# First modulation as columns on TensorE, norm and skip on the Hyena filters, and a new load order in front of a hybrid encoder layer

## The chip, the cores and the metric

The kernel runs on one core of one Trainium2 chip. The metric is the device time of one execution in microseconds (us), less is better. The kernel before takes 1514.09 us, the median of three runs (1512.0 to 1516.69).

## What is computed

One layer of an encoder trunk over 1024 tokens of width 1024, cut to what matters here:

```
sh1, sc1, g1, sh2, sc2, g2 = split(silu(c) @ mod_w + mod_b)     # six vectors of 1024
u  = rms_norm(x) * (1 + sc1) + sh1
p  = u @ w_in                     # 28 tiles of 128 columns and 24 gate columns
SSD, NA, mLSTM, Hyena each work on their columns of p
x  = x + g1 * (concat(groups) @ w_out)
x  = x + g2 * SwiGLU(rms_norm(x) * (1 + sc2) + sh2)
out = rms_norm(x)
# Hyena: per order o two filters h = sin-MLP(features) @ w3 * decay,
# divided by the root of their square sum; y = fft-convolution(z, h) + skip * z
```

Only the first two of the six vectors, sh1 and sc1, are needed in front of u. All is fp32. A product of the projection is made as three fp32r matmuls, hi·hi, lo·hi and hi·lo, of operands that are split into a rounded part and the rest.

## The kernel before

The program is one stream per engine, in order; the framework sorts each engine's instructions by priority and by when their operands come, and semaphores hold an instruction back until its operands are there. What stands behind a waiting instruction on its engine waits too.

The part in front is one function, `start` (L400 to L468), with the generator `hyena_filters` (L719) run beside it:

- **First modulation.** `mod_w` for sh1 and sc1 comes as four quarters q of 2 MB, each in four tiles `mw` of 512 KB. For q = 0 to 2 VectorE (DVE) multiplies a 128x512 slice of a tile by one element of silu(c) per partition and adds it to `acc` (L422, L424: 24 instructions); for q = 3 ScalarE (ACT) multiplies (L427) and GpSimd (POOL) adds (L429). Then 16 TensorE (PE) transposes (L449) and four reductions on DVE (L451) sum over the partitions and leave the result as columns in `mod1`.
- **Norm and split.** Eight 512 KB tiles of x come after all of `mw`. ACT squares them (L439), `rsqrt` on the sums makes the factors, L444 multiplies. For each half h of the tokens and each of eight column tiles k, PE transposes four 128x128 blocks (L462), ACT applies the modulation (L464, `tm`), and `split` makes `hhi` and `hlo` (L235, L239), the latter on DVE or POOL by turns.
- **Projection.** `gemm_t` (L485) makes one column tile of p transposed, 2 halves of 24 matmuls (L495, `gps`); `w_group` (L471) loads and splits the weights (`raw`, `whi`, `wlo`). The first three groups of tiles belong to Hyena: `conv3` (L512) and `to_natural` (L525, `nps`, `z`) follow them.
- **Filters.** `hyena_mlp` (L693) makes h2 with two sines (DVE polynomials L684 to L689, ACT L690). `hyena_filters` makes, for each order o and block j, a product with w3 on PE (L738, `fps`), times the decay `dc` on DVE (L743, `hf`), its square on ACT (L746), a sum of the two directions on DVE (L747), a matmul with ones that adds up the squares (L748, `nps`), and the sum and difference `hp`, `hm` on DVE (L751, L752). `dft16_fwd` (L536) runs a first stage of the transform on DVE (L550 to L607), `emit` the second on PE (L765, L767, `kps`), and then DVE multiplies each of the spectra by the norm (L769) and adds the skip to the real ones (L771) before they are stored in `kspec`.

The Hyena convolution (`fps` of L792) begins when z and the spectra are there. Behind it come the other groups, the second modulation (L1500, `mxw`), the out projection, the feed-forward part (`ffn`, products `X`, `Y`, `Z` of L1606 with combinations on DVE) and the last norm.

Of the kernel before, what the change touches and what calls it, by code (L numbers as in the profile page):

```python
# [9 lines left out]
F32 = mybir.dt.float32  # L10
F32R = mybir.dt.float32r
AF = mybir.ActivationFunctionType
ALU = mybir.AluOpType
# [7 lines left out]
NK = 8  # L21
# [197 lines left out]
class Net:  # L219


    def __init__(self, nc, tc, d, out):
        self.nc, self.tc, self.d, self.out = nc, tc, d, out
        self.n = 0

# [60 lines left out]
def build(nc, tc, d, out, dbg=None, dump=None):  # L286
    K = Net(nc, tc, d, out)
    with ExitStack() as es:
# [58 lines left out]
        with ExitStack() as e2:  # L347
# [3 lines left out]
            with ExitStack() as e3:  # L351
                fl = Tags(rpool("fl", e3), n4=2, n2=8, yk=3, n1=2, tab=3, ks=3)
                hyena_mlp(K, fl)
                K.wp = Tags(pool("wp", e2), raw=3, whi=2, wlo=2)
                with ExitStack() as e4:
                    hf = hyena_filters(K, fl)
                    w0 = []
                    start(K, hp, Tags(pool("st", e4), tm=2), lambda: next(hf), lambda: w0.extend(w_group(K, G_HY + 2, first=False)))
                for _ in hf:
                    pass  # L360
# [39 lines left out]
def start(K, hp, sp, between, mid):  # L400
# [3 lines left out]

    accs, mts = {}, {}
    slots = [f"{t}{k}" for k in range(NK) for t in ("hhi", "hlo")]
    for qs in ((0, 3), (1,), (2,)):
        if qs == (2,):
            between()
        for q in qs:  # L410
            accs[q] = sp.tile([P, 512], F32, f"acc{q}")
        for k in range(NK):
            for q in qs:

                acc, c = accs[q], K.cond[:, k:k + 1]
                if k % 2 == 0:
                    mts[q] = hp.tile([P, 2, 512], F32, name="mw", tag=slots.pop(0))
                    nc.sync.dma_start(mts[q], d["modw1"][q, :, k:k + 2].rearrange("p k s c -> p k (s c)"))
                w = mts[q][:, k % 2]
                if q < 3:  # L420
                    if k == 0:
                        V.tensor_scalar_mul(acc, w, c)  # L422
                    else:
                        V.scalar_tensor_tensor(acc, in0=w, scalar=c, in1=acc, op0=ALU.mult, op1=ALU.add)  # L424
                else:
                    t = acc if k == 0 else sp.tile([P, 512], F32, "pr", bufs=2)
                    nc.scalar.activation(t, w, AF.Identity, scale=c)  # L427
                    if k > 0:
                        nc.gpsimd.tensor_tensor(acc, acc, t, op=ALU.add)  # L429
    ss = sp.tile([P, 8], F32, "ss")  # L430
    xs = []
    for g in range(4):
        xt = K.wp.tile([P, NK, 288], F32, ("whi", "wlo")[g % 2], name="x").rearrange("p a b -> p (a b)")
        for i in range(2):
            x = xt[:, i * D:(i + 1) * D]
            n = 2 * g + i
            nc.sync.dma_start(x, d["x"][n * P:(n + 1) * P, :])
            jk = K.so.tile([P, D], F32, "st", name="jk")
            nc.scalar.activation(jk, x, AF.Square, accum_out=ss[:, n:n + 1])  # L439
            xs.append(x)  # L440
    def norm(h):
# [4 lines left out]
    for q in (0, 3, 1, 2):  # L446
        ps = K.pm.tile([P, 512], F32, tag="m", name="psm")
        for n in range(4):
            nc.tensor.transpose(ps[:, n * P:(n + 1) * P], accs[q][:, n * P:(n + 1) * P], K.ident)  # L449
        mc = sp.tile([P, 2, 2], F32, "mc", bufs=2)  # L450
        V.tensor_reduce(mc, ps.rearrange("p (s k x) -> p s k x", s=2, k=2), axis=AX.X, op=ALU.add)  # L451
        mv = K.mod1.rearrange("p (s k) -> p s k", s=2)[:, :, 2 * q:2 * q + 2]
        V.tensor_tensor(mv, mc, K.pc[:, PC_MODB:PC_MODB + 16].rearrange("p (s k) -> p s k", s=2)[:, :, 2 * q:2 * q + 2], op=ALU.add)
        V.tensor_scalar_add(mv[:, 1], mv[:, 1], 1.0)
    K.hhi = [hp.tile([P, L], F32R, name=f"hhi{k}", tag=f"hhi{k}") for k in range(NK)]
    K.hlo = [hp.tile([P, L], F32R, name=f"hlo{k}", tag=f"hlo{k}") for k in range(NK)]
    for h in range(2):
        norm(h)
        for k in range(NK):
# [3 lines left out]
            t = sp.tile([P, 512], F32, tag="tm") if k % 2 else K.so.tile([P, 512], F32, "st", name="tm")  # L463
# [21 lines left out]
def gemm_t(K, whi, wlo, j):  # L485
# [3 lines left out]
    pss = []  # L489
    for h in range(2):  # L490
# [3 lines left out]
        for n, (w, x, k) in enumerate(seq):  # L494
            nc.tensor.matmul(ps, lhsT=w[:, k, c], rhs=x[k][:, t], start=n == 0, stop=n == len(seq) - 1)  # L495
# [196 lines left out]

def hyena_mlp(K, sp):  # L693
# [7 lines left out]
    for c in range(2):  # L701
        nc.sync.dma_start(w2[64 * c:64 * c + 64], d["w2"])

# [15 lines left out]
def hyena_filters(K, sp):  # L719
# [4 lines left out]
    for o in range(2):  # L724
        w3 = sp.tile([P, 512], F32, "w3")
        for c in range(2):
            nc.sync.dma_start(w3[64 * c:64 * c + 64], d["w3"][:, o * 512:(o + 1) * 512])
        hp = sp.tile([P, 8, 256], F32, "hp")
        hm = sp.tile([P, 8, 256], F32, "hm")
        pn = K.pm.tile([P, 512], F32, "m", name="nps")[:, :256]  # L730
        pss = {}
        for j in (0, 4, 1, 5, 2, 6, 3, 7):
            if j < 4:

                for b in (j, j + 4):
                    r = slice(64 * (b // 4), 64 * (b // 4) + 64)
                    pss[b] = K.pm.tile([P, 512], F32, "m", name="fps")
                    nc.tensor.matmul(pss[b], lhsT=h2[r, j * P:(j + 1) * P], rhs=w3[r], start=True, stop=True)  # L738
            ps = pss[j]
            dc = sp.tile([P, 1, 256], F32, "n1", name="dc")  # L740
            nc.sync.dma_start(dc[:, 0], d["c_decay"][:, j])
            hf = sp.tile([P, 2, 256], F32, "n2", name="hf")
            V.tensor_tensor(hf, ps.rearrange("p (a b) -> p a b", a=2), dc.broadcast_to([P, 2, 256]), op=ALU.mult)  # L743
            hff = hf.rearrange("p a b -> p (a b)")
            s1 = sp.tile([P, 512], F32, "n2", name="s1")
            nc.scalar.activation(s1, hff, AF.Square)  # L746
            V.tensor_tensor(s1[:, 0:256], s1[:, 0:256], s1[:, 256:512], op=ALU.add)  # L747
            nc.tensor.matmul(pn, lhsT=K.ones, rhs=s1[:, 0:256], start=j == 0, stop=j == 7)  # L748
            if j == 0:
                G.memset(hf[0:1, 1, :], 0.0)  # L750
# [4 lines left out]
        fsc = K.rsqrt(sp, pn, [P, 256], 1.0, "fn")  # L755
        skip = sp.tile([P, 256], F32, "skip")
        nc.sync.dma_start(skip, d["skip"][:, 256 * o:256 * o + 256].broadcast_to([P, 256]))
        for q, (src, la, lb) in enumerate(((hp, 0, 1), (hm, 1, 0))):

            def emit(k, y):  # L760
# [821 lines left out]
def ffn(K, sp, S, at):  # L1582
# [134 lines left out]
    for f in range(NF):  # L1717
# [24 lines left out]
        if f < KH:  # L1742
            V.tensor_tensor(x[:, 0], x[:, 1], x[:, 0], op=ALU.subtract)
# [14 lines left out]
        if f < KH:  # L1758
            V.tensor_tensor(y[:, 1], a[:, 0:H], a[:, H:L], op=ALU.subtract)
# [118 lines left out]
```

## Time and profile before

| | us |
|---|---|
| median of three runs | 1514.09 (1512.0 to 1516.69) |
| profiled execution | 1520.79 |
| its span | 1518.9 |
| PE busy in the span | 1389.5 (91%) |
| DVE busy in the span | 1118.4 (74%) |
| ACT busy in the span | 542.5 (36%) |
| POOL busy in the span | 90.9 (6%) |
| first matmul of the projection | 85.82 |
| first matmul of the Hyena convolution | 218.86 |

The span runs from the first to the last recorded instruction of the profiled execution; that execution's own time is 1.9 us longer. A busy share is an average over the whole span. PE is busy for 36.90 of the first 85.80 us and for 1232.16 of the 1300 us behind 218.9. The granted clock is 1.00 for TensorE at its full speed of 2.4 GHz and 0.50 for the lower level of 1.2 GHz; a value between them is a stretch that has some of both.

### The profile page before, as it was taken

How to read it: one execution, taken by the hardware profiler on the slowest of the kernel's cores; microseconds unless marked ns; L12 is line 12 of the kernel's file. 1: busy time of each engine (PE TensorE's matmuls, PEld its weight loads, DVE VectorE, ACT ScalarE, POOL GpSimd, SP SyncE). 2: the span in 40 equal slices, each digit the busy share in tenths (PEclk: the TensorE clock that was granted, in tenths of full speed). 3: DMA queues.
4: the chain of work that ended last, by engine and by line, in shares of the span. 5: the costliest groups of instructions: out<-in, count | busy, mean ns of one | idle time of the engine just before them, and what ended most of it. 6: DMA issues, size and time to landing. Idle time of an engine off the chain costs nothing.

```text
span 1518.9 us, 19510 instructions
## 1 busy us (share of the span) xinstructions
PE 1389.5 (91%) x6717; PEld 1115.8 (73%) x6717; DVE 1118.4 (74%) x2123; ACT 542.5 (36%) x973; POOL 90.9 (6%) x143
## 2 busy tenths in 40 slices
PE   2589989998998998999998999999999999999995
PEld 0366768776787767877776777887778878888884
DVE  7999977887756684687865458378777887557588
ACT  2522221232142342333545766322222222434352
POOL 2110000000101231320000000000000000000000
PEclk9789999999998999989999999999999999999998
DMA  6634366577662324476435448677776776977762
GB/s 248 196 101 146 121 198 217 181 240 222 205 195 93 114 84 154 118 250 223 151 102 180 146 164 285 230 258 249 254 246 218 234 266 239 331 236 244 238 221 110
DMA packets 160598, 300.31 MB, mean 198 GB/s; under 512 B 27871, under 2 KB 72831, under 8 KB 160500
## 3 DMA queue, kind: packets, MB, share of 16 engines
q1 hardware_dynamic: 137204, 271.77, 54.6%
q10 hardware_dynamic: 22688, 25.99, 4.8%
q0 software_dynamic: 608, 1.31, 0.3%
q8 instruction: 53, 0.87, 0.2%
q14 instruction: 45, 0.37, 0.1%
HBM read 221.12 MB, written 77.89 MB: 197 GB/s over the span
## 4 chain that ended last, share of the span: by engine, by line
PE 59%; DVE 14%; DMA 9%; issue 3%; ACT 1%; POOL 1%; SPq 0%; POOLq 0%; DVEq 0%; ACTq 0%
PE Z L1606 8%; PE X L1606 6%; PE dx L1844 6%; PE Y L1606 5%; PE gps L495 5%; PE gps L507 4%; PE dz L1844 4%; PE dy L1844 4%; PE gps L1556 3%; DMA mxw<-modw 3%; DMA wu<-wu 2%; PE nS L1429 2%; PE ops L1556 1%; PE nS L1407 1%; DVE wlo L239 1%
## 5 line engine op out<-in xcount | busy, mean ns | idle before, releaser
L495 PE MATMUL gps<-hhi,whi 128*128 128x512 f32 x320 | 130.3, 407 | 3.8 <-ACT nt L531 3.8
L495 PE MATMUL gps<-hlo,whi 128*128 128x512 f32 x320 | 128.9, 403 | 0.0
L495 PE MATMUL gps<-hhi,wlo 128*128 128x512 f32 x320 | 128.4, 401 | 0.0
L239 DVE TENSOR_TENSOR dl<-dr,dh 128x1024 fp32r<-128x1024 f32 x77 | 93.5, 1221 | 37.4 <-ACT dh L233 25.2
L233 ACT CAST dh<-dr 128x1024 fp32r<-128x1024 f32 x77 | 80.4, 1052 | 104.6 <-PE dz L1844 30.0
L1606 PE MATMUL Z<-hp,wgh 128*128 128x512 f32 x352 | 95.8, 402 | 1.0 <-ACT ps L1661 0.9
L507 PE MATMUL gps<-whi,hhi 128*128 128x256 f32 (+1 forms) x256 | 76.8, 300 | 1.5 <-ACT z L531 1.5
L1606 PEld LDWEIGHTS Z<-hp,wgh 128*128 128x128 f32 x352 | 63.6, 188 | 19.2 <-ACT ps L1661 4.7
L507 PE MATMUL gps<-whi,hlo 128*128 128x256 f32 (+1 forms) x256 | 76.8, 300 | 0.0
L507 PE MATMUL gps<-wlo,hhi 128*128 128x256 f32 (+1 forms) x256 | 76.3, 298 | 0.0
L495 PEld LDWEIGHTS gps<-hhi,whi 128*128 128x128 f32 x320 | 60.5, 189 | 19.3 <-ACT nt L531 5.0
L233 ACT CAST T3h<-wu 128x1024 fp32r<-128x1024 f32 x22 | 23.1, 1052 | 132.0 <-PE Y L1606 121.1
L495 PEld LDWEIGHTS gps<-hhi,wlo 128*128 128x128 f32 x320 | 60.2, 188 | 13.7 <-issue 1.6
L495 PEld LDWEIGHTS gps<-hlo,whi 128*128 128x128 f32 x320 | 60.4, 189 | 12.2 <-issue 0.8
L1500 DVE SCALAR_TENSOR_TENSOR mxacc<-mxw,cond,mxacc 128x512 f32<-128x512 f32 x56 | 41.9, 748 | 32.4 <-DMA mxw<-modw 32.2
L1606 PE MATMUL X<-A,t4s 128*128 128x512 f32 x264 | 63.6, 390 | 0.1
L1606 PEld LDWEIGHTS X<-A,t4s 128*128 128x128 f32 x264 | 49.5, 188 | 10.8 <-DVE uv L1745 0.5
L507 PEld LDWEIGHTS gps<-whi,hhi 128*128 128x128 f32 x256 | 49.9, 195 | 3.1 <-ACT z L531 1.9
L1606 PE MATMUL Y<-AS,T3h 128*128 128x512 f32 x176 | 45.5, 400 | 7.3 <-DVE uv L1741 7.3
L1844 PE MATMUL dx<-dh,dl 128*128 128x512 f32 x132 | 51.4, 389 | 0.0
L1844 PE MATMUL dx<-dh 128*128 128x512 f32 x132 | 51.4, 389 | 0.0
L1844 PE MATMUL dx<-dl,dh 128*128 128x512 f32 x132 | 51.4, 389 | 0.0
(521 smaller groups left out, 3511.2 us busy)
## 6 DMA issues: line engine op xcount, KB each, us to landing
wg<-wg SPq DMA_DIRECT2D x44, 512.0 KB
mxw<-modw SPq DMA_DIRECT2D x64, 256.0 KB
raw<-w_in SPq DMA_DIRECT2D x28, 512.0 KB
dr<-wd SPq DMA_DIRECT2D x55, 256.0 KB
psd<-ps SPq DMA_DIRECT2D x22, 512.0 KB
psr<-psd SPq DMA_DIRECT2D x22, 512.0 KB
wu<-wu SPq DMA_DIRECT2D x22, 512.0 KB
ad<-a SPq DMA_DIRECT2D x22, 512.0 KB
```

Source lines behind the costliest of these rows:

```text
L233: nc.scalar.copy(hi, src)
L239: e.tensor_tensor(lo, src, hi.bitcast(F32), op=ALU.subtract)
L495: nc.tensor.matmul(ps, lhsT=w[:, k, c], rhs=x[k][:, t], start=n == 0, stop=n == len(seq) - 1)
L507: nc.tensor.matmul(ps, lhsT=x[k][:, t], rhs=w[:, k, :N], start=n == 0, stop=n == len(seq) - 1)
L1407: nc.tensor.matmul(pb[:, :nk], lhsT=qt[r, i], rhs=ktv[r, r0:r0 + nr, f * 24:f * 24 + 40], start=True, stop=True)
L1429: nc.tensor.matmul(pb[:, 448:512], lhsT=pT[:w * 40, n], rhs=vw[:w * 40, n, c:c + 64], start=n == 0, stop=n == len(chunks) - 1)
L1500: V.scalar_tensor_tensor(acc, in0=mt, scalar=K.cond[:, k:k + 1], in1=acc, op0=ALU.mult, op1=ALU.add)
L1556: K.nc.tensor.matmul(ps, lhsT=l, rhs=r, start=n == 0, stop=n == 5)
L1606: nc.tensor.matmul(ps, lhsT=w[a][:, k], rhs=x[k][b], start=start and n == 0, stop=n == 11, skip_group_check=not start)
L1844: nc.tensor.matmul(acc[i], lhsT=a[:, 0, ts], rhs=b[:, 1], start=first and m == 0, stop=final and m == 2, skip_group_check=n in (2, 3, 5, 6))
```

## The change

Four parts.

1. **Modulation on TensorE.** The accumulation on DVE, ACT and POOL is gone. For each quarter q, 32 matmuls (128 in all) take a 128x128 block of `mw` as the stationary operand and one column of silu(c) as the moving one, and write one column of `pc` each; a reduction over eight columns and the bias follow.
2. **Load order and halves.** On the load queue: w3 with the other filter weights, then x0 to x3, the whole decay as one transfer of 1 MB, the 16 tiles of `mw`, x4 to x7, w_in. The norm of half 0 stands ahead of the filters, that of half 1 behind the splits of half 0. `mid` hands its weights back, and half 0 of the column tiles j = 0 and 1 is multiplied before half 1 is transposed (`K.half`). All `hlo` are made on DVE, `tm` has three buffers.
3. **Filters.** Sum and difference of the two directions' weights are formed once per order (`ws`), so that the product with them is already hp or hm; the squares of both go to the matmul with ones, twice as many of them, and the factor 1.0 of `rsqrt` is 2.0. Norm and skip are applied to the filters, and the spectra are copied out by ACT.
4. **Feed-forward.** The two subtractions into `x` and the store `td` stand at the end of a column tile in the source.

```diff
-    for qs in ((0, 3), (1,), (2,)):
...
-                if q < 3:
-                    if k == 0:
-                        V.tensor_scalar_mul(acc, w, c)
-                    else:
-                        V.scalar_tensor_tensor(acc, in0=w, scalar=c, in1=acc, op0=ALU.mult, op1=ALU.add)
...
+    load_x(0)
+    nc.sync.dma_start(K.dc, d["c_decay"])
...
+            nc.sync.dma_start(mt, d["modw1"][q, :, 2 * n:2 * n + 2].rearrange("p k s c -> p k (s c)"))
+    load_x(1)
+    norm(0)
+    between()
+    for q in range(4):
+        pc = K.pm.tile([P, 512], F32, tag="m", name="psm")[:, 0:32]
+        for k in range(NK):
+            for c in range(4):
+                n = c * NK + k
+                nc.tensor.matmul(pc[:, n:n + 1], lhsT=mts[q][k // 2][:, k % 2, c * P:(c + 1) * P], rhs=K.cond[:, k:k + 1],
+                                 start=True, stop=True)
...
-        norm(h)
+        if h == 1:
+            norm(1)
...
-            K.split(K.hhi[k][:, c], K.hlo[k][:, c], t, "dve", "dve" if k % 2 else "pool")
+            K.split(K.hhi[k][:, c], K.hlo[k][:, c], t, "dve", "dve")
         if h == 0:
-            mid()
+            w = mid()
+            K.half = {j: gemm_t(K, *w, j, 1) for j in range(2)}
...
+        V.tensor_tensor(ws[:, 0], w3[:, 0:256], w3[:, 256:512], op=ALU.add)
+        V.tensor_tensor(ws[:, 1], w3[:, 0:256], w3[:, 256:512], op=ALU.subtract)
...
-            V.tensor_tensor(s1[:, 0:256], s1[:, 0:256], s1[:, 256:512], op=ALU.add)
-            nc.tensor.matmul(pn, lhsT=K.ones, rhs=s1[:, 0:256], start=j == 0, stop=j == 7)
+            for q in range(2):
+                nc.tensor.matmul(pn, lhsT=K.ones, rhs=s1[:, q], start=j == 0 and q == 0, stop=j == 7 and q == 1)
...
-            V.tensor_tensor(hp[:, j], hf[:, 0], hf[:, 1], op=ALU.add)
-            V.tensor_tensor(hm[:, j], hf[:, 0], hf[:, 1], op=ALU.subtract)
...
+        for q in range(2):
+            V.tensor_tensor(h[:, q], h[:, q], fsc[:, None, :].broadcast_to([P, 8, 256]), op=ALU.mult)
+            if q == 0:
+                V.tensor_tensor(hp[0:1, 0], hp[0:1, 0], skip, op=ALU.add)
...
-                V.tensor_tensor(ks, ps, fsc, op=ALU.mult)
-                if q == 0:
-                    V.tensor_tensor(ks, ks, skip, op=ALU.add)
+                nc.scalar.copy(ks, ps)
...
-        if f < KH:
-            V.tensor_tensor(x[:, 0], x[:, 1], x[:, 0], op=ALU.subtract)
...
-        if f < KH:
-            V.tensor_tensor(x[:, 1], y[:, 0], x[:, 0], op=ALU.subtract)
-            nc.sync.dma_start(K.td[f], x)
...
+            V.tensor_tensor(x[:, 0], x[:, 1], x[:, 0], op=ALU.subtract)
+            V.tensor_tensor(x[:, 1], y[:, 0], x[:, 0], op=ALU.subtract)
+            nc.sync.dma_start(K.td[f], x)
```

How the change moves the instructions, at three places. A row is line, operation, what is written and read, the shape, and how many in a row.

PE in front, before, from the first product of the filters' last block to the projection: `psm` is the modulation, `nps` the filters' square sums, `tps` the transposes of x.

```order
L738 MATMUL fps<-w_347,h_258 128x512 x2
L748 MATMUL nps<-s_396,ones 128x256
L449 MATMUL psm<-ident,acc_282 128x128 x3
L748 MATMUL nps<-s_410,ones 128x256
...
L449 MATMUL psm<-ident,acc_450 128x128 x4
L462 MATMUL tps<-ident,x 128x128 x48
L765 MATMUL kps<-yk,tab 128x256 x2
L462 MATMUL tps<-ident,x 128x128 x8
...
L495 MATMUL gps<-hhi_532,whi_634 128x512
```

PE in front, as changed, from the first transposes to half 1.

```order
L456 MATMUL tps<-ident,x 128x128 x16
L745 MATMUL fps<-ws,h_262 128x512 x2
L754 MATMUL nps<-s_364,ones 128x256 x2
...
L441 MATMUL psm<-cond,mw 128x1 x43
L754 MATMUL nps<-s_414,ones 128x256 x2
L441 MATMUL psm<-cond,mw 128x1 x85
L456 MATMUL tps<-ident,x 128x128 x16
L490 MATMUL gps<-hhi_566,whi_654 128x512
...
L490 MATMUL gps<-hhi_573,wlo_655 128x512
L456 MATMUL tps<-ident,x 128x128 x32
```

The filters of order 0 now stand ahead of the modulation, the modulation's 128 matmuls stand as one block ahead of the projection, and 48 matmuls of half 0 stand ahead of the transposes of half 1.

DVE as changed, from the last split of half 0 to the first of half 1: `h` are the filters, `fnr` their norm, `ln1r` the norm of the second half of x, `n` the transform's first stage.

```order
L240 TENSOR_TENSOR wlo_655<-raw_656,whi_654 128x8x128
L240 TENSOR_TENSOR hlo_581<-tm,hhi_573 128x512
...
L255 TENSOR_TENSOR fnr<-fnr,fnt 128x256
L766 TENSOR_TENSOR h<-h,fnr 128x2048
L766 TENSOR_TENSOR h<-h,fnr 128x2048
L255 TENSOR_TENSOR ln1r<-ln1r,ln1t 128x4
L769 TENSOR_TENSOR h<-h,skip 1x256
L423 TENSOR_SCALAR x<-x,ln1r 128x1024 x4
L548 TENSOR_TENSOR n_824<-h 128x1024
L549 TENSOR_TENSOR n_825<-h 128x1024
L236 CAST hhi_566<-tm 128x512
```

The same place on DVE before.

```order
L444 TENSOR_SCALAR x<-x,ln0r 128x1024 x4
...
L444 TENSOR_SCALAR x<-x,ln1r 128x1024
L235 CAST hhi_532<-tm 128x512
L235 CAST hhi_533<-tm 128x512
L444 TENSOR_SCALAR x<-x,ln1r 128x1024
L239 TENSOR_TENSOR hlo_541<-tm,hhi_533 128x512
```

Two of the four products with `ln1r` stood between the splits of half 0; now all four stand behind both products of the filters with their norm, and the transposes of half 1 need them.

DVE in a column tile of the feed-forward part, before: `uv` and `a` combine the products X and Y, `sx` are the two subtractions of part 4, L1743 and L1751.

```order
L1741 TENSOR_TENSOR uv<-Y,psr 128x512
L1745 TENSOR_TENSOR uv<-X,uv 128x512
L1743 TENSOR_TENSOR sx<-sx 128x512
L1751 TENSOR_TENSOR sx<-sx 128x512
L1747 TENSOR_TENSOR uv<-Y,uv 128x512
```

The same place as changed.

```order
L1751 TENSOR_TENSOR uv<-Y,psr 128x512
L1753 TENSOR_TENSOR uv<-X,uv 128x512
L1764 TENSOR_TENSOR sx<-sx 128x512
L1765 TENSOR_TENSOR sx<-sx 128x512
L1755 TENSOR_TENSOR uv<-Y,uv 128x512
```

The two subtractions stand at the same place of the engine's order in both.

## Rows read from the trace of the kernel before

**Rows 1.** Stretches in us: busy (count) per engine, granted clock, DMA share, GB/s.

```profile
0.00:85.80 85.80, 36.90 (x128) 20.60 (x129) 75.17 (x136) 36.65 (x59) 18.78 (x19) 0.84 0.63 212
...
98.00:213.10 115.10, 106.03 (x452) 80.25 (x450) 103.61 (x217) 27.24 (x42) 0.30 (x1) 0.96 0.41 129
...
218.90:1518.90 1300.00, 1232.16 (x6063) 1002.45 (x6062) 924.03 (x1748) 469.70 (x860) 67.81 (x121) 0.98 0.62 204
...
12.00:16.00 4.00, 0.00 (x0) 0.00 (x0) 4.00 (x3) 1.39 (x2) 3.69 (x3) 1.00 1.03 420
```

**Rows 2.** PE's timeline in front: start us, us, instruction, idle time before it.

```profile
30.10 2.15 PE L738 MATMUL fps<-w,h 64*128 64x512 f32 x4 [10.21 <-ACT h L690]
85.82 0.58 PE L495 MATMUL gps<-hhi,whi 128*128 128x512 f32 x1
```

**Rows 3.** The chain that ended last, from 186 to 224 us: start us, us, what.

```profile
189.59 2.78 PE gps L495 x12
192.36 1.29 PE kps L765 x6
...
213.73 5.12 PE gps L507 x38
218.86 0.50 PE fps L792 x2
```

**Rows 4.** Groups of DVE by shape, 0 to 218.9 us: busy us, mean ns, idle before.

```profile
L424 DVE SCALAR_TENSOR_TENSOR acc<-mw,cond,acc 128x512 f32<-128x512 f32 x21 | 18.6, 884 | 0.3
L769 DVE TENSOR_TENSOR ks<-kps,fnr 128x256 f32<-128x256 f32 x36 | 14.8, 418 | 9.2 <-PE kps L767 5.1 <-DMA kspec<-ks 3.7 <-PE kps L765 0.2
L239 DVE TENSOR_TENSOR wlo<-raw,whi 128x1024 fp32r<-128x1024 f32 x10 | 13.0, 1322 | 0.3 <-ACT whi L233 0.2
...
L771 DVE TENSOR_TENSOR ks<-ks,skip 128x256 f32<-128x256 f32 x18 | 8.4, 476 | 0.0
...
L239 DVE TENSOR_TENSOR hlo<-tm,hhi 128x512 fp32r<-128x512 f32 x8 | 5.4, 678 | 0.0
...
L553 DVE TENSOR_TENSOR n<-hp 128x1024 f32<-128x1024 f32 x2 | 2.4, 1216 | 0.0
```

**Rows 5.** Weight loads of the filters' products, 30 to 33 and 41 to 46 us: ns min/median/max.

```profile
L738 PEld LDWEIGHTS fps<-w,h x4: 284/308/334, 30.1 to 30.3; 64*128 64x128 f32 x4
...
L738 PEld LDWEIGHTS fps<-w,h x4: 183/184/186, 42.1 to 43.7; 64*128 64x128 f32 x4
```

**Rows 6.** PE's timeline from 480 to 492 us, fp32 matmuls of 32 columns and the next ones.

```profile
483.77 0.97 PE L1251 MATMUL dcp<-mwi,selr 128*128 128x32 f32 x4
484.55 0.56 PE L507 MATMUL gps<-whi,hhi 128*128 128x256 f32 x1
...
488.09 0.97 PE L1046 MATMUL eps<-sac,tri 128*128 128x32 f32 x8
488.89 0.61 PE L1046 MATMUL eps<-sac,ones 128*128 128x32 f32 x4
```

**Rows 7.** The same places, and a run of narrow matmuls: busy time and clock by stretch.

```profile
483.60:484.50 0.90, 0.90 (x6) 0.90 (x6) 0.00 (x0) 0.38 (x1) 0.90 (x5) 0.50 0.44 137
488.00:489.00 1.00, 1.00 (x12) 1.00 (x11) 0.00 (x0) 0.29 (x2) 0.00 (x0) 1.00 0.23 80
662.00:663.00 1.00, 1.00 (x10) 0.89 (x9) 0.62 (x2) 0.42 (x1) 0.46 (x2) 1.00 1.06 391
663.00:664.00 1.00, 1.00 (x12) 0.93 (x13) 0.53 (x2) 0.00 (x0) 0.00 (x0) 0.96 1.06 424
664.00:665.00 1.00, 1.00 (x7) 0.77 (x6) 0.94 (x4) 0.00 (x0) 0.00 (x0) 0.50 1.13 401
```

**Rows 8.** PE's timeline from 660 to 672 us, the run of narrow matmuls.

```profile
659.89 0.71 PE L1335 MATMUL mpi<-mpv,mqk 64*128 64x130 f32 x4
...
662.11 1.55 PE L1341 MATMUL mpa<-mkv,msd 128*128 128x65 f32 x12
```

**Rows 9.** PE's waits from 950 to 1310 us: in total, times, longest, us.

```profile
PE Y L1606 <- DVE uv L1741: 7.3, 9, 1.2
```

More of the change, by code (lines that the diff above doesn't have):

```diff
@@ L224, in __init__ @@
         self.n = 0
+        self.half = {}
     def first(self):
@@ L357, in build @@
                     w0 = []
-                    start(K, hp, Tags(pool("st", e4), tm=2), lambda: next(hf), lambda: w0.extend(w_group(K, G_HY + 2, first=False)))
+                    start(K, hp, Tags(pool("st", e4), tm=3), lambda: next(hf), lambda: w0.extend(w_group(K, G_HY + 2, first=False)) or w0)
                 for _ in hf:
@@ L403, in start, with load_x, norm @@
     V = nc.vector
-    accs, mts = {}, {}
-    slots = [f"{t}{k}" for k in range(NK) for t in ("hhi", "hlo")]
-    for qs in ((0, 3), (1,), (2,)):
[L408 to L419, printed above, removed]
-                if q < 3:
-                    if k == 0:
-                        V.tensor_scalar_mul(acc, w, c)
-                    else:
-                        V.scalar_tensor_tensor(acc, in0=w, scalar=c, in1=acc, op0=ALU.mult, op1=ALU.add)
[L425 to L429, printed above, removed]
     ss = sp.tile([P, 8], F32, "ss")
     xs = []
[L432 to L437, printed above, removed]
+    def load_x(h):
+        for g in (2 * h, 2 * h + 1):
+            xt = K.wp.tile([P, NK, 288], F32, ("whi", "wlo")[g % 2], name="x").rearrange("p a b -> p (a b)")
+            for i in range(2):
+                x = xt[:, i * D:(i + 1) * D]
+                n = 2 * g + i
+                nc.sync.dma_start(x, d["x"][n * P:(n + 1) * P, :])
+                xs.append(x)
+    def norm(h):
+        for n in range(4 * h, 4 * h + 4):
             jk = K.so.tile([P, D], F32, "st", name="jk")
-            nc.scalar.activation(jk, x, AF.Square, accum_out=ss[:, n:n + 1])
-            xs.append(x)
-    def norm(h):
+            nc.scalar.activation(jk, xs[n], AF.Square, accum_out=ss[:, n:n + 1])
         r = K.rsqrt(sp, ss[:, 4 * h:4 * h + 4], [P, 4], D, f"ln{h}")
@@ L482, in w_group, with gemm_t @@
     return whi, wlo
-def gemm_t(K, whi, wlo, j):
+def gemm_t(K, whi, wlo, j, n=2):
     nc = K.nc
     c = slice(j * P, (j + 1) * P)
-    pss = []
-    for h in range(2):
+    pss = K.half.pop(j, [])
+    for h in range(len(pss), n):
         t = slice(h * 512, (h + 1) * 512)
@@ L493, in gemm_t @@
         seq = [(w, x, k) for k in range(NK) for w, x in ((whi, K.hhi), (whi, K.hlo), (wlo, K.hhi))]
-        for n, (w, x, k) in enumerate(seq):
-            nc.tensor.matmul(ps, lhsT=w[:, k, c], rhs=x[k][:, t], start=n == 0, stop=n == len(seq) - 1)
+        for m, (w, x, k) in enumerate(seq):
+            nc.tensor.matmul(ps, lhsT=w[:, k, c], rhs=x[k][:, t], start=m == 0, stop=m == len(seq) - 1)
         pss.append(ps)
@@ L690, in sin_layer, with filter_weights @@
     nc.scalar.activation(o, u, AF.Sin)
+def filter_weights(K, sp, o):
+    w3 = sp.tile([P, 512], F32, "n2", name="w3")
+    for c in range(2):
+        K.nc.sync.dma_start(w3[64 * c:64 * c + 64], K.d["w3"][:, o * 512:(o + 1) * 512])
+    return w3
 def hyena_mlp(K, sp):
@@ L702, in hyena_mlp @@
         nc.sync.dma_start(w2[64 * c:64 * c + 64], d["w2"])
+    K.dc = sp.tile([P, 8, 256], F32, "dc")
+    K.w3 = [filter_weights(K, sp, 0)]
     ps = K.pm.tile([P, 512], F32, "m", name="fps")
@@ L724, in hyena_filters @@
     for o in range(2):
[L725 to L729, printed above, removed]
+        w3 = K.w3.pop() if o == 0 else filter_weights(K, sp, o)
+        ws = sp.tile([P, 2, 256], F32, "ws")
+        V.tensor_tensor(ws[:, 0], w3[:, 0:256], w3[:, 256:512], op=ALU.add)
+        V.tensor_tensor(ws[:, 1], w3[:, 0:256], w3[:, 256:512], op=ALU.subtract)
+        h = sp.tile([P, 2, 8, 256], F32, "h")
+        hp, hm = h[:, 0], h[:, 1]
         pn = K.pm.tile([P, 512], F32, "m", name="nps")[:, :256]
```

35 lines of the change are left out of this document (17 added, 18 removed).

## The prediction

> **What bounds the kernel now.** I read the busy time by stretch first. Behind 218.9 us, where the Hyena convolution begins, PE is busy for 1232 of 1300 us at a clock of 0.98 [rows 1]: PE sets the time there, and what comes later or earlier at 218.86 comes so at the end, if the order behind stays. In the dense stretch from 98 to 213.1 PE has 106.0 of 115.1 us and DVE 103.6 [rows 1]: both are nearly full. In front of 85.8 us it is DVE, 75.2 of 85.8, against PE's 36.9 [rows 1]. So the front is where something can be had. The timeline of PE gives its two marks, the first product of the filters at 30.10, after a sine, and the first matmul of the projection at 85.82 [rows 2]; the chain that ended last gives the third, the convolution at 218.86 [rows 3]. The change is worth what it moves that third mark by.
>
> **Sum, step 1: the filters' start.** At 30.10 PE had waited 10.2 us for the second sine [rows 2]. Eleven of the 24 accumulations stand on DVE ahead of it, 0.884 each [rows 4], 9.7 us, and go. Some of them filled time in which DVE would wait for PE and ACT in this chain anyway, and four products with the first norm now fill the same time. I take half, 5 us of gain, h2 at 25 (bounds 20 and 30; I think of 22 to 30). The loads do not hold it: up to the last `mw` tile they are 11.6 MB in all, 28 us at 420 GB/s [rows 1] from about 8 us on, so the last one is there at 36, before the stream below asks for it.
>
> **Step 2: filters of order 0 ahead of the stream.** A record of 256 columns takes 0.215 us (six in 1.29 [rows 3]), one fp32 matmul is two records, so 0.43, and 0.86 with 512 columns. Eight products and 14 of the 16 square sums stand ahead: 8 x 0.86 + 14 x 0.43 = 12.9 us. The old sums were eight of 0.43 in front; eight more are 3.4 us. Weight loads there took 0.308 us at 30 us and 0.184 at 42 [rows 5]: the clock was at its lower level first, for which I add 3. The stream starts at 25 + 12.9 + 3 = 41 (38 to 46). DVE keeps up, with one multiplication for each block in place of four instructions.
>
> **Step 3: the stream.** 128 fp32 matmuls with one moving column are 256 pairs of a weight load and a matmul. No row has one column; the nearest have 32. At full clock eight such records stand 0.80 us before the next group, 0.100 each; at half clock four stand 0.78 us before the next, 0.195 each [rows 6, 7]. Below 0.100 I do not go, since each pair still loads 128x128 weights. The bounds are 25.6 us at full clock and 49.9 at half.
>
> Which clock? A run of narrow matmuls began at 659.89 [rows 8]. PE is busy for 1.00 of each of three stretches, and the clock is 1.00, 0.96 and then 0.50 [rows 7]: it fell while PE had no gap. The stream is narrower still. So I take full clock for about as long as that run kept it, 4 us, or 40 pairs, and half for 216: 42.1 us. With 1.2 us for the two square sums in between, it ends at T = 41 + 4 + 42.1 + 1.2 = 88 (80 to 95). Before, the first projection matmul came at 85.82.
>
> The Trainium skill, page "TensorE: Matmul & The Clock Gate", section "What's actually happening", says that the clock follows how busy PE has been; a PE without gaps would keep it. Its section "LDWEIGHTS (loading the stationary operand)" gives columns/1.2 ns for a weight load, 107 ns for 128, which by an estimate from that page makes the stream 256 x 0.107 = 27.4 us and the sum some 1504. The rows speak against both: the clock fell at a busy PE [rows 7], and a weight load took 0.308 at one level and 0.184 at the other [rows 5].
>
> **Step 4: from T to a dense PE.** Most modulated tiles need the last quarter of the modulation. Behind it stand, on DVE, seven casts and seven `hlo` of half 0 (0.42 to 0.68 each [rows 4], 7.7 to 9.5) with `wlo` (1.32) among them: the projection begins at about T+10. Its 48 matmuls take 11.1 (0.232 each, twelve in 2.78 [rows 3]), to T+21. Meanwhile DVE has two products of 128x2048, not in the trace: bounded by 1.22, if size did not count, and four times that; twice the 1.216 of 128x1024 [rows 4], 2.43 each, is nearest. With the four products of the second norm and two first transform steps that is 11 us, to T+22. The transposes of half 1 wait for it; eight splits follow, to T+33. I take T+34, PE partly idle for the last 13 us.
>
> **Step 5: the dense stretch.** What PE has left then: 214 projection matmuls x 0.232 = 49.6; 64 transform matmuls x 0.43 = 27.5; filters of order 1, 8 x 0.86 + 16 x 0.43 = 13.8, of which 3.4 is new; 48 transposes and 32 narrow matmuls at 0.135 (38 in 5.12 [rows 3]), 10.8: 102. DVE loses here 34 multiplications by the norm (0.418), 17 additions of the skip (0.476) [rows 4] and 24 instructions of order 1's filters (of the first one's shape): 32 us; it gains 5 for the two norm products and weight sums, and some 18 of the first transform and splits come behind T+34 now: 95 in place of 103.6. ACT gains 36 copies of about 0.41, 15 us onto 27 [rows 1], covered. PE was idle for 9 of 115 us; with less on DVE I take 3. The convolution begins at T + 34 + 102 + 3 = T+139 = 227, against 218.86: **8 us later**.
>
> **Step 6: the rest.** The feed-forward subtractions keep their place among DVE's instructions, and so does what follows them; PE's waits for Y, 7.3 us in nine [rows 9], stay. Cost 0, and no cover is needed. Between the convolution and the out projection a few instructions trade places without more work; from there on no engine's order changes. The stores of spectra move nothing else: their queue stays ACT's.
>
> The profiled execution took 1520.8 us; it would take 1529. It lies 6.7 above the median of 1514.1, so I carry the difference: **1522 us**. About 0.3%, 4.5 us, is what a measurement of this kernel can tell from no change.
>
> **Rivals.**
>
> *The clock holds, or the load is as short at either level (faster).* The stream takes 25.6 us, T = 68, the convolution at 207, 12 us earlier: 1502. For it: PE has no gap. Against: the fall of [rows 7]. It decides at T = 80, a stream of about 38 us, 0.148 for a pair, between the two prices of [rows 6].
>
> *The clock comes and goes in the stream, or a pair at half clock is nearer 0.16 (no change).* Four loads are few, and the first carries a switch of type. 40 x 0.100 + 216 x 0.16 = 38.6 and T = 81, the convolution at 220, 1 us later: 1515. The same time would follow from a stretch behind T that is 7 us denser than in steps 4 and 5.
>
> *The tail is worse (slower by more).* If half 1 waits for a fuller chain of ACT and DVE, and the first 48 matmuls run at the clock that the stream left, 11 us more for them, the convolution is at about 238: 1533. For it: after the stream the clock is low, and PE has a gap of 10 us.
>
> *The move in the feed-forward part does something.* By the order it does not; a profile in which the waits for Y change would say otherwise.
>
> **How the numbers follow.** Chances: forecast 0.50, clock holds 0.20, no change 0.20, worse tail 0.10. The forecast's own range, T from 80 to 95, is 1514 to 1529; a third of it lies at less than 4.5 us. Faster: 0.20 and 0.07 from the edge of the third case, 0.27. Same: 0.13 of the third and 0.10 of the forecast's lower end, 0.23. Slower: 0.50. The range that holds 8 in 10 takes in the rival at 1502, with its bound of 2 us below, and ends at 1530, which leaves the worse tail out.
>
> **What would show it.** Right: the 256 records in a block from about 41 to 88 us, the clock at 0.50 for most of it, the first projection matmul near 98, the convolution near 227, spectra copied by ACT, the waits for Y as before. Wrong: a stream that ends before 80, by its clock or by shorter pairs; a dense stretch well under 102 us of PE; a shift at 218.86 that is not found at the end.

## The result

The changed kernel takes 1571.45 us, the median of four runs, against 1514.92 for the kernel before, also four: 1.0367 times as long (95% interval 1.0332 to 1.0401). It is slower, as forecast, but by 56.5 us and not by 8, far outside the range. The profiled execution took 1570.05 us with a span of 1568.1, 49.2 more than the span of before; its marks follow. (A record below is one matmul or weight load as the trace lists it; an fp32 matmul has two of each.)

The page of the changed kernel: busy time by engine, and the clock in 40 slices of 39.2 us.

```profile
PE 1463.2 (93%) x6989; PEld 1182.4 (75%) x6989; DVE 1069.8 (68%) x2019; ACT 552.8 (35%) x1003; POOL 65.2 (4%) x126
...
PEclk8559999999999899999999999999999999999998
```

DVE lost 48.6 us, as the change wanted, and PE gained 73.7. The second and third slice of the clock read 5: PE ran at its lower level from 39 to 118 us.

Busy time by stretch, changed kernel: the filters of order 0, the block of the modulation with the last square sums, from there to the dense part, and, as one stretch, from the first projection matmul to the convolution. The second listing is that last stretch in the kernel before.

```profile
24.70:53.30 28.60, 27.02 (x45) 11.87 (x46) 6.27 (x10) 5.04 (x8) 0.00 (x0) 0.53 0.74 298
53.30:109.50 56.20, 56.20 (x262) 55.84 (x260) 2.48 (x11) 4.59 (x6) 0.00 (x0) 0.50 0.00 1
109.50:137.50 28.00, 22.24 (x97) 16.76 (x97) 27.31 (x51) 15.72 (x25) 0.00 (x0) 0.78 0.14 39
116.40:261.60 145.20, 131.54 (x576) 101.19 (x577) 119.63 (x211) 57.30 (x105) 0.00 (x0) 0.96 0.42 132
```

```profile
85.80:218.70 132.90, 120.28 (x529) 92.57 (x527) 119.19 (x240) 36.19 (x55) 4.31 (x4) 0.96 0.41 132
```

PE is busy for 27.0 of 28.6 us and then for all of 56.2, and the clock is 0.53 and 0.50. The weight loads show where it fell: 0.184 us in the first products and 0.310 in the next ones, the two durations of [rows 5].

```profile
L745 PEld LDWEIGHTS fps<-ws,h x4: 182/184/186, 24.7 to 24.9; 64*128 64x128 f32 x4
L745 PEld LDWEIGHTS fps<-ws,h x6: 285/310/334, 29.4 to 37.6; 64*128 64x128 f32 x6
```

DVE, which set the front before [rows 1], does 8.8 us of work in these 84.8. Beside the block it mostly waits for it, in order: each of the four reductions of a quarter (`mc`) stands ahead of work that needs none of them, the filters' norm `fnr` among it, whose operand is there from 74.4 on. The two products with that norm come only at 122. DVE's waits from 53.3 to 109.9 us, and the two products:

```profile
DVE mc L444 <- PE psm L441: 48.9, 4, 14.8
...
L766 DVE TENSOR_TENSOR h<-h,fnr x2: 2285/2288/2291, 122.1 to 124.4; 128x2048 f32<-128x2048 f32 x2
```

PE's timeline of the changed kernel, the marks of [rows 2] first:

```profile
24.75 1.13 PE L745 MATMUL fps<-ws,h 64*128 64x512 f32 x4 [2.06 <-ACT h L685]
...
45.41 2.07 PE L745 MATMUL fps<-ws,h 64*128 64x512 f32 x2
47.41 2.07 PE L754 MATMUL nps<-s,ones 128*128 128x256 f32 x4
...
53.29 18.34 PE L441 MATMUL psm<-cond,mw 128*128 128x1 f32 x86
71.49 2.05 PE L754 MATMUL nps<-s,ones 128*128 128x256 f32 x4
73.34 36.27 PE L441 MATMUL psm<-cond,mw 128*128 128x1 f32 x170
...
116.46 0.79 PE L490 MATMUL gps<-hhi,whi 128*128 128x512 f32 x1 [3.33 <-ACT whi L234]
```

The first projection matmul comes 30.6 us later than at 85.82 [rows 2]. The convolution's first matmul and the block's weight loads, grouped by line (ns min/median/max, first and last start):

```profile
L802 PE MATMUL fps<-yk,tab x36: 377/379/794, 261.6 to 446.1; 128*128 128x256 f32 x36
```

```profile
L441 PEld LDWEIGHTS psm<-cond,mw x256: 333/333/337, 52.9 to 109.2; 128*128 128x128 f32 x128
```

By its line the convolution began at 218.7 before; it is 42.9 us later. So 30.6 of the 49.2 us are lost ahead of the projection, 12.3 between it and the convolution, and 6.3 behind.

### The profile page after: what moved, and what is told of

The parts are those of the page before. It is cut to its first block, busy times and chain, and to the rows that moved or that the text cites. A ratio compares the mean times of both kernels' runs of the same rounds, so it can differ in the third digit from the quotient of the medians.

```text
span 1568.1 us, 19935 instructions
## 1 busy us (share of the span) xinstructions
PE 1463.2 (93%) x6989; PEld 1182.4 (75%) x6989; DVE 1069.8 (68%) x2019; ACT 552.8 (35%) x1003; POOL 65.2 (4%) x126
## 4 chain that ended last, share of the span: by engine, by line
PE 66%; DVE 14%; DMA 9%; issue 4%; ACT 3%; POOL 2%; SPq 0%; POOLq 0%; DVEq 0%; ACTq 0%
PE Z L1616 8%; PE gps L490 8%; PE dx L1852 6%; PE X L1616 5%; PE Y L1616 5%; PE gps L502 4%; PE dz L1852 4%; PE psm L441 3%; PE dy L1852 3%; PE gps L1566 3%; DMA wu<-wu 2%; DMA mxw<-modw 2%; PE nS L1439 2%; PE nps L754 2%; PE ops L1566 1%
## 5 line engine op out<-in xcount | busy, mean ns | idle before, releaser
L441 PEld LDWEIGHTS psm<-cond,mw 128*128 128x128 f32 x256 | 55.1, 333 | 0.4
L441 PE MATMUL psm<-cond,mw 128*128 128x1 f32 x256 | 54.6, 351 | 0.0
L502 PEld LDWEIGHTS gps<-whi,hlo 128*128 128x128 f32 x256 | 51.0, 199 | 1.1 <-issue 0.5
```

Source lines behind the costliest of these rows:

```text
L441: nc.tensor.matmul(pc[:, n:n + 1], lhsT=mts[q][k // 2][:, k % 2, c * P:(c + 1) * P], rhs=K.cond[:, k:k + 1], start=True, stop=True)
L502: nc.tensor.matmul(ps, lhsT=x[k][:, t], rhs=w[:, k, :N], start=n == 0, stop=n == len(seq) - 1)
```

## Experiments

The theories: **A**, PE runs the modulation's block and the filters at its lower clock, because so little moves through the array, and the block stands ahead of the projection in order. **B**, the new order (loads, filters first, halves) costs it. **C**, the doubled square sums and the norm ahead of the transform cost it. The experiments ran on three chips where the kernel before takes 1518 to 1519 us; ratios, with their 95% intervals, are to it. They are given as recorded and differ from the quotient of the two medians by 0.35% at most. The changed kernel itself was not run there; its 1.0367 is from the result. What has a single run has no interval.

### Which part of the change

*The changed kernel with the modulation on DVE again:*

```diff
-                nc.tensor.matmul(pc[:, n:n + 1], lhsT=mts[q][k // 2][:, k % 2, c * P:(c + 1) * P], rhs=K.cond[:, k:k + 1],
+                V.scalar_tensor_tensor(acc, in0=w, scalar=c, in1=acc, op0=ALU.mult, op1=ALU.add)
+            nc.tensor.transpose(pc[:, n * P:(n + 1) * P], acc[:, n * P:(n + 1) * P], K.ident)
```

> The changed kernel with part 1 undone: the first modulation is accumulated on DVE again (32 multiply-adds, four groups of transposes), parts 2 to 4 stay. Theory A (the block of 256 one-column records on PE, 54 us at the lower clock, is what the path waits for): DVE is busy for only 6 of the 29 us of the filters, so the 32 accumulations (about 22 us) fit beside them; the first projection matmul comes at about 65 to 72 in place of 116, the time falls by about 45 us to 1525 (1512 to 1537). Theory B (the new load order, the filters ahead on PE and the projection by halves cost most of it): the first projection matmul stays behind 90 and the time above 1545.

1532.63 us, ratio 1.007 (1.0039 to 1.0102). The first projection matmul comes at 67.6, as A expected. Part 1 is some 3% of the 3.7%. The rest is real too: the convolution starts at 222.5, after a longer stretch.

```profile
67.60:222.50 154.90, 136.20 (x583) 103.92 (x583) 123.53 (x219) 57.39 (x103) 0.00 (x0) 0.94 0.38 122
```

*The kernel before with part 1 alone:*

```diff
-                        V.scalar_tensor_tensor(acc, in0=w, scalar=c, in1=acc, op0=ALU.mult, op1=ALU.add)
+                nc.tensor.matmul(ps[:, n:n + 1], lhsT=mts[q][k // 2][:, k % 2, c * P:(c + 1) * P], rhs=K.cond[:, k:k + 1],
+                                 start=True, stop=True)
```

> The kernel before with part 1 alone: the modulation as 128 one-column matmuls, loads, filters and halves as before. Theory A: PE gets a block of about 54 us behind most of the filters' products, the first projection matmul comes at 100 to 110 in place of 85.8, the convolution some 15 to 25 us later: 1530 to 1540. Theory B: part 1 by itself takes 21 us off DVE, which is the busy engine in front, and the block lies beside it: the time is that of before or some us less, 1500 to 1517.

1559.97 us, ratio 1.0235 (1.0177 to 1.0293; the medians alone give 1.027): more than the 1530 to 1540 of A. Norm, transposes and splits of both halves follow the block here, 32.7 us from 99.2 on. The block by its line, and its stretch:

```profile
L436 PE MATMUL psm<-cond,mw x256: 212/353/353, 44.1 to 99.2; 128*128 128x1 f32 x128
...
44.10:99.20 55.10, 55.10 (x259) 54.92 (x257) 4.35 (x17) 4.62 (x7) 0.00 (x0) 1.00 0.23 77
```

The 256 records take 55 us, 0.215 each, the price of the lower level as in the changed kernel; why the clock column says 1.00 all the same is told at the end. The first projection matmul comes at 131.9; from there to the convolution at 262.6 it is 130.7 us, against 132.9 before: nothing behind the first projection matmul is longer. B falls as the main cause. Part 2 alone was not tried.

*The kernel before with part 3 alone,* and *with part 4 alone:*

```diff
+        for q in range(2):
+            V.tensor_tensor(h[:, q], h[:, q], fsc[:, None, :].broadcast_to([P, 8, 256]), op=ALU.mult)
...
-                V.tensor_tensor(ks, ps, fsc, op=ALU.mult)
...
+                nc.scalar.copy(ks, ps)
```

> The kernel before with part 3 alone: sums of the weights, norm and skip on the filters, spectra copied by ACT, twice the square sums. Theory A: this part takes load off DVE (some 35 us over both orders against 10 added) where DVE and PE are both nearly full and adds 7 us of matmuls: the convolution starts 5 to 15 us earlier, 1500 to 1510. Theory C (the doubled square sums and the norm in front of the transform are a part of the loss): the same or slower, 1514 to 1525.

1525.11 us, ratio 1.0022 (0.9993 to 1.0051): no gain, where A expected one. The first projection matmul comes 7 us earlier, at 78.6, and the convolution at 219.3 as before:

```profile
78.60:219.30 140.70, 125.12 (x549) 97.40 (x548) 111.21 (x186) 49.77 (x92) 4.75 (x3) 0.96 0.44 138
```

DVE has 8 us less in that stretch than before and PE 4.8 more. C explains a few us at most.

```diff
-        if f < KH:
-            V.tensor_tensor(x[:, 0], x[:, 1], x[:, 0], op=ALU.subtract)
         product(X, w["T3"], A["S3"], False)
```

> The kernel before with part 4 alone, the two subtractions at the end of a column tile in the source. All theories: the order on every engine is as before, so the time is that of before within 5 us, and PE's waits for Y in the feed-forward part stay at about 7 us. A change of more than 5 us would say that the move does something that the order does not show.

1518.61 us in one run, beside 1518.97 for the kernel before. PE's waits for Y, here and in the changed kernel:

```profile
PE Y L1606 <- DVE uv L1741: 7.5, 9, 1.6
```

```profile
PE Y L1616 <- DVE uv L1751: 7.1, 9, 1.7
```

The move does nothing, as its order said [rows 9].

### What holds the clock down

*128 moving columns in place of one, same loads, same number of matmuls (the two loops change places, so that the columns are written in rising order):*

```diff
-        for k in range(NK):
-            for c in range(4):
+        for c in range(4):
+            for k in range(NK):
...
-                nc.tensor.matmul(pc[:, n:n + 1], lhsT=mts[q][k // 2][:, k % 2, c * P:(c + 1) * P], rhs=K.cond[:, k:k + 1],
-                                 start=True, stop=True)
+                nc.tensor.matmul(ps[:, n:n + 128], lhsT=mts[q][k // 2][:, k % 2, c * P:(c + 1) * P],
+                                 rhs=K.cond[:, k:k + 1].broadcast_to([P, 128]), start=True, stop=True)
```

> The changed kernel with the column of silu(c) repeated to 128 moving columns: each matmul of the block writes 128 equal columns, of which the next one overwrites all but the first. Weight loads and matmuls are as many as before. Theory A (the one moving column leaves the array nearly unused, and the clock follows the use): the granted clock rises within the block, a record takes about 0.11 to 0.13 in place of 0.212, the block about 30 to 35 us in place of 54, the first projection matmul comes near 95 in place of 116.5 and the time falls by some 20 us. Theory D (the clock is low for what went ahead of the block, or fp32 weight loads hold it low, whatever the width): it stays at 0.50, a record takes 0.21 or more, the block 54 us or more, and the time does not fall.

1530.12 us, ratio 1.0067 (1.0032 to 1.0102): more work on PE, and 3% of the time comes back, twice the 20 us that A gave. Timeline and stretches of this run:

```profile
56.62 28.08 PE L442 MATMUL psm<-cond,mw 128*128 128x128 f32 x250
```

```profile
54.00:60.00 6.00, 6.00 (x41) 5.67 (x40) 2.63 (x4) 3.34 (x7) 0.00 (x0) 0.78 0.01 3
60.00:66.00 6.00, 6.00 (x57) 6.00 (x55) 5.90 (x10) 2.06 (x5) 0.00 (x0) 1.00 0.00 0
```

0.112 us for a record in place of 0.213, at a clock of 1.00. The block ends at 84.5 in place of 109.5, 25 us earlier. The convolution comes 37 us earlier, at 224.8, and the other 12 us are not the block's: the framework also ordered the instructions anew. DVE now does the filters' norm and the first transform steps beside the block, 26.2 us of work in its 27.9, and eight transform records stand ahead of the projection. How much of the 12 us is this order, and how much the clock behind the block (0.50 up to 122 us in the changed kernel, 1.00 here), this run does not separate.

*Operands exchanged, one column of weights and 512 moving columns:*

```diff
+            nc.tensor.matmul(pr, lhsT=K.cond[:, k:k + 1], rhs=mts[q][k // 2][:, k % 2], start=k == 0, stop=k == NK - 1)
```

> The changed kernel with the operands of the modulation exchanged: the column of silu(c) is the stationary operand (one column of weights), 512 columns of the weights move, eight matmuls add up in one row of 512; four small matmuls per quarter turn the row into columns. 64 records of 512 columns in place of 256 of one. Theory A1 (the width of the moving operand sets the clock): it rises within the block, which takes 28 to 33 us. Theory A2 (the used share of the array sets it; one of 128 columns of weights is used): the clock stays at 0.50, the block takes 54 to 60 us, and the time is about that of the changed kernel.

1542.03 us in one run, beside 1517.84. The clock rises with one of 128 weight columns in use:

```profile
75.86 7.03 PE L439 MATMUL psr<-mw,cond 128*1 128x512 f32 x16
```

```profile
78.00:84.00 6.00, 5.23 (x15) 1.18 (x14) 5.97 (x13) 0.00 (x0) 0.00 (x0) 1.00 0.00 0
```

16 records in 7.03 are 0.44 each, the price at full clock. A2 falls in the form it had: here the clock was 1.00 with 127 of 128 columns of weights unused. The four quarters together took longer than the 28 to 33 us of A1, from 53.8 to 93.4: the clock was lower at first and once more in the second (0.72 from 66 to 72), and PE waited 0.8 to 1.3 us in each for DVE to copy the row.

*Filter products over 128 rows in place of 64:*

```diff
-                    nc.tensor.matmul(pss[b], lhsT=h2[r, j * P:(j + 1) * P], rhs=ws[r].rearrange("p a b -> p (a b)"),
+                    nc.tensor.matmul(pss[b], lhsT=h2[:, j * P:(j + 1) * P], rhs=ws[:, b // 4].rearrange("p a b -> p (a b)"),
```

> The changed kernel with the products of the filters contracted over all 128 rows (the weights of the other half are zeros) in place of 64; same number of records, same columns. Theory A2 (the clock follows the used share of the array): the clock rises within the filters of order 0, which take 15 to 19 us in place of 28.6; the block of the modulation starts near 41 to 45, falls to 0.50 again, and all marks behind it are 10 to 13 us earlier. Theory D (the clock is low for another reason): the filters stay at 0.50 and 28 us, and nothing moves.

1547.68 us in one run, beside 1517.84. Timeline, then stretches:

```profile
36.86 1.02 PE L747 MATMUL fps<-ws,h 128*128 128x512 f32 x2
37.72 1.07 PE L756 MATMUL nps<-s,ones 128*128 128x256 f32 x4
...
40.35 15.59 PE L441 MATMUL psm<-cond,mw 128*128 128x1 f32 x86
```

```profile
25.50:40.30 14.80, 14.78 (x44) 8.72 (x45) 6.19 (x10) 4.41 (x7) 0.52 (x1) 0.88 1.03 420
40.40:93.60 53.20, 53.20 (x261) 52.84 (x260) 2.48 (x11) 5.22 (x7) 0.33 (x1) 0.53 0.10 36
```

The block's own records, before and behind the fall of the clock (busy, count, clock, DMA share, GB/s):

```profile
40.40:43.30 2.90, 2.90 (x28) 1.00 1.02 395
43.40:53.40 10.00, 10.00 (x49) 0.50 0.20 72
```

A step of the filters takes 1.8 us in place of 4.0, the filters 14.8 in place of 28.6, and the one-column block, which starts at full clock here, falls to the lower level. By their starts its one-column records stand 0.112 us apart up to 43.3 and 0.213 from 43.4 on: the same record has both prices, so the clock sets them and not the record's shape. Records and columns are as many as before and PE has no gap in either run from 27.4 us on; only the rows that move differ, and with 128 the clock rose where with 64 it stayed down. This is also the cleanest trial of A: PE's order is that of the changed kernel up to the convolution, and DVE does as little beside the block (2.48 us). The block ends 15.9 us earlier, the convolution, at 244.6, 17.0 earlier, more than the 10 to 13 expected.

*One quarter only, in PE's idle time of the kernel before:*

```diff
+                        nc.tensor.matmul(pq[:, n * NK + k:n * NK + k + 1], lhsT=w[:, n * P:(n + 1) * P], rhs=c, start=True, stop=True)
```

> The kernel before with the one quarter of the modulation that ACT and POOL made (q = 3) as 32 one-column matmuls, ahead of the filters, where PE has nothing to do for 12 us; the other quarters stay on DVE, and POOL has nothing to add in front. Theory A: 64 records at 0.21 are 13.6 us in PE's idle time from 18 to 31; DVE's accumulations take about 0.70 in place of 0.884 without POOL beside them, so the first projection matmul comes 3 to 6 us earlier: 1509 to 1517 where the kernel before takes 1519. Theory B' (every such record on PE is paid, wherever it stands): 10 to 14 us slower.

1524.73 us, ratio 1.0054 (1.0022 to 1.0087): slower, where A expected a gain. The block took 13.81 us, as expected, in idle time; but DVE's reduction of it stood ahead of the second sine in DVE's order, and DVE waited for the whole block:

```profile
DVE mc L454 <- PE psq L425: 12.0, 1, 12.0
```

Neither theory had that: not the records were paid but the wait, put in front of work that was ready. It is the wait that DVE has beside the block of the changed kernel too.

### The repair, and what it leaves

*Both clock edits together* (the two diffs above):

> The changed kernel with both clock edits together: filter products over 128 rows and 128 moving columns in the block. Theory A (the loss of the change is the lower clock in front): the filters take 15 us, the block 28, both at a clock of 1.00; the block ends near 70 in place of 109.5, the convolution starts near 207 to 212 (in the run with the wide block alone it started 140 us behind the block's end), and the time is 1505 to 1515 where the kernel before takes 1518: the change turns from 57 us slower to as fast or a little faster. Theory E (the wide block gained by the other order of the instructions behind it, and the filters' gain does not add to it): 1525 or more.

1515.93 us, ratio 0.998 (0.996 to 1.0001). The whole loss is gone with two edits that add work. Timeline, stretches, and the two products with the filters' norm:

```profile
25.36 3.75 PE L748 MATMUL fps<-ws,h 128*128 128x512 f32 x4 [2.15 <-ACT h L686]
...
32.77 1.02 PE L748 MATMUL fps<-ws,h 128*128 128x512 f32 x2
...
43.26 28.08 PE L442 MATMUL psm<-cond,mw 128*128 128x128 f32 x250
```

```profile
25.40:41.50 16.10, 16.10 (x45) 9.33 (x46) 6.26 (x10) 4.41 (x7) 0.59 (x1) 1.00 1.03 420
43.30:71.20 27.90, 27.90 (x252) 27.90 (x251) 26.28 (x55) 8.94 (x17) 0.00 (x0) 1.00 0.09 31
75.70:211.90 136.20, 125.21 (x576) 99.40 (x577) 101.57 (x177) 52.56 (x96) 0.00 (x0) 0.99 0.48 150
...
L769 DVE TENSOR_TENSOR h<-h,fnr x2: 2284/2289/2294, 47.9 to 50.2; 128x2048 f32<-128x2048 f32 x2
```

The block ends at 71.2, 38.3 us earlier than in the changed kernel, and the convolution starts at 211.9, 49.7 earlier. So 38 of the 43 us that the convolution had lost are the filters and the block, at the higher clock; the other 11.4 lie behind the block, where DVE's order is another one: 26.3 us of its work lie beside the block in place of 2.5, the two products with the norm at 48 in place of 122. That order came with the edit and was not tried by itself. (The first products, 3.75 us for four records where a later pair takes 1.02, were still at the lower level, though the column reads 1.00.)

*Two quarters on DVE, and that with the squares added on DVE again:*

```diff
+        if q < 2:
+            acc = sp.tile([P, 512], F32, tag="tm", name="acc")
...
-            for q in range(2):
-                nc.tensor.matmul(pn, lhsT=K.ones, rhs=s1[:, q], start=j == 0 and q == 0, stop=j == 7 and q == 1)
+            V.tensor_tensor(s1[:, 0], s1[:, 0], s1[:, 1], op=ALU.add)
+            nc.tensor.matmul(pn, lhsT=K.ones, rhs=s1[:, 0], start=j == 0, stop=j == 7)
```

> The same with two of the four quarters of the modulation accumulated on DVE, which is idle for 22 us beside the filters; the block on PE is 128 records. Theory A: the block ends near 56 to 60, everything behind it 10 to 14 us earlier than with both clock edits alone, 1493 to 1505. Against it: DVE takes 11 us more in front, and what it does there delays the filters' products by as much; then it is no better than with both edits.

> The same again, with the two directions' squares added on DVE (0.42 us, 16 times) ahead of the matmul with ones, as before the change, so that PE has 16 square sums less, 0.43 each. If the doubled square sums cost their 3.4 us in the dense stretch and as much in front: 3 to 7 us faster than the version with two quarters on DVE. If DVE is what the stretch waits for: the same or slower.

Two quarters on DVE: 1514.7 us, ratio 0.9986 (0.9959 to 1.0012), not the 1493 to 1505 of A. The block ends at 61.7, 9.5 earlier than with both edits, but the convolution, at 207.3, is only 4.6 earlier. From the first projection matmul to there DVE has 115.6 us, 14 more than with both edits. With the squares on DVE: 1510.73 us, ratio **0.9952 (0.9932 to 0.9973)**, half a percent faster than the kernel before. Its convolution starts at 200.8, 6.5 earlier; in time the two versions' intervals overlap.

*Without the early half:*

```diff
-            K.half = {j: gemm_t(K, *w, j, 1) for j in range(2)}
```

> The changed kernel without the early product of half 0 (column tiles 0 and 1 are multiplied once both halves are transposed). The loads and everything in front of it stay. If the early half fills PE while DVE makes half 1: about 8 to 11 us slower, 1578 to 1584, with PE idle behind the block. If it only delays the transposes of half 1: the same or some us faster.

1573.58 us in one run, beside 1518.41 (a quotient of 1.0363, where the changed kernel has 1.0367). The first projection matmul moves from 116.5 to 135.3 and the convolution from 261.6 to 268.1, and the end does not show it. The early half is neither the loss nor a gain that can be seen.

## Why the prediction was wrong

The sign and the place were right: the block on PE, at the lower clock, ahead of the projection. The size was not. Steps 2, 3 and 5 failed, by 12.3, 9 and 19 us; 6 of the 19 are those that step 4 had too many.

- **Step 1** (filters from 25): 24.75. Right, though half of 9.7 us was a choice and not worked out.
- **Step 2** (12.9 us of filters at full clock, 3 more for a low start): 28.6 us. The forecast took the clock for low at first and let it rise, as it had between 30 and 42 us before [rows 5]. It did the opposite: full in the first products, low from the next ones on, 0.53 over the stretch. Before, PE had this:

```profile
36.57 3.31 PE L738 MATMUL fps<-w,h 64*128 64x512 f32 x6
39.81 0.70 PE L748 MATMUL nps<-s,ones 128*128 128x256 f32 x2
40.44 1.12 PE L738 MATMUL fps<-w,h 64*128 64x512 f32 x2
41.49 0.70 PE L748 MATMUL nps<-s,ones 128*128 128x256 f32 x2
```

  Six records of products stood there without a square sum between them, the first four two at a time, one on each half of the rows; the last of the six, from 39.3, took 0.59 us in place of 1.0 to 1.2. Here single 64-row products alternate with square sums. That this is why the clock rose there is not tried; that the rows matter is: 128 of them gave 14.8 us. The price was low too: a 64-row product stands 1.05 us before the next group at full clock (40.44 to 41.49), not 0.86. Step 2 is 12.3 us of the miss.
- **Step 3** (47 us with 4 at full clock): 56.2. The direction, that a busy PE with narrow matmuls loses its clock, was right and is now shown by the wide block. The run that it was read from had a gap of 0.28 us at 660.9; this block has none in 56 us. Mis-sized were the start, since the clock was low already, and the pair: 0.213 us where 0.195 from four loads [rows 6] was taken. 9 us.
- **Step 4** (projection at T+10, dense from T+34): T+7 and T+28. 6 us too much. The first ten records of the projection ran at the lower clock, as the rival of the worse tail had it.
- **Step 5** (105 us: 102 of PE's work and 3 in which it is idle): 124.1 from 137.5 to 261.6, with PE busy for 112.9 and idle for 11.2. That stretch and the first 5.6 us of the projection:

```profile
137.50:261.60 124.10, 112.92 (x497) 87.65 (x497) 99.08 (x176) 46.81 (x88) 0.00 (x0) 0.97 0.46 145
...
116.40:122.00 5.60, 5.15 (x11) 3.25 (x12) 5.60 (x14) 3.91 (x8) 0.00 (x0) 0.51 0.31 91
```

  Six of these 19 us are those that step 4 had too many, 8 are the idle time, 5 the work. The idle time was to shrink from 9 with the load of DVE. The two long waits for the transform on DVE did go, but waits in Hyena's own chain (`nt`, `acc`) grew. PE's longest waits, first of the changed kernel from 137 us on, then of before from 98:

```profile
PE gps L490 <- ACT nt L526: 5.0, 3, 2.4
PE nps L525 <- DVE acc L516: 3.4, 1, 3.4
```

```profile
PE kps L765 <- DVE yk L593: 3.5, 2, 2.7
PE kps L765 <- DVE yk L550: 2.9, 1, 2.9
PE nps L530 <- DVE acc L521: 2.4, 1, 2.4
...
PE gps L495 <- ACT nt L531: 1.4, 3, 0.7
```

  From the first projection matmul on, PE is busy for 11.3 us more than before (131.5 against 120.3) with 47 records more: 32 transposes of half 1 (4.3 at 0.135 [rows 3]), 16 records of square sums (3.4), and a slow start, the clock being 0.51 up to 122. DVE has 119.6 against 119.2: what part 3 saved there, moved work replaced. These splits are worked out, not tried.
- **Step 6** (nothing behind): the feed-forward move costs nothing, right. But the end is 6.3 us later than the convolution's delay. From the convolution's start to the end, the 14 profiled executions of this case take 1293.6 to 1307.6 us: before 1300.2, changed 1306.5, part 3 alone 1304.2, but the wide block 1299.9 and both clock edits 1298.0, which have parts 2 to 4 too. Where the 6.3 arises stays open; that the parts cost it is not shown.

The last 7 of the 56.5 us are no step's: the profiled execution of before lay 5.9 above the median of its kernel, a difference that the forecast carried on, and that of the changed kernel 1.4 below.

The rival with the clock held needed full clock on a one-column block, which lasted for 3 us of it in the run with 128-row filters. Its other form, a load as short at either level, falls by the 0.112 and 0.213 of that run. The rule weighed in step 3, that the clock follows how busy PE has been (the Trainium skill, page "TensorE: Matmul & The Clock Gate", section "What's actually happening"), does not hold here if busy is PE's busy share: that was 1.00 for 56.2 us at 0.50. The 107 ns for a load of 128 columns, an estimate by the formula of the Trainium skill, same page, section "LDWEIGHTS (loading the stationary operand)", fit the 0.112 for a record at full clock and not the 0.213 at half.

## What to carry to other kernels

A PE without a gap is not a PE at full clock: price a block of narrow matmuls at the lower level, with what stands around it, until a row shows otherwise. Where such a block must be, try to let more columns or rows move, even ones that nobody reads: with 128 columns in place of one, and as many records, this block took 28 us in place of 54. And work that leaves the busiest engine is gained only if both engines then have something to do: some 20 us that left DVE came back as 56 on PE, ahead of the projection, while DVE waited for 48.9 of them, from 74 us on with ready work behind the wait in its order.

## What had not been expected

Rows of zeros and repeated columns, which add nothing to the result, raised the clock: 0.53 to 0.88 in the filters, 0.50 to 1.00 in the block. And the clock column of a profile reads 1.00 up to the first change that an execution records: in the kernel before it says 1.00 at 30 us, where weight loads took 0.308 us in place of 0.184 [rows 5], and with part 1 alone it says 1.00 over a block that took 55 us. The duration of a weight load, or of a block whose price is known, is the better witness there.
